# One order of products for all still weights, and one place in SBUF for each kind of weight slab

## The chip, the core and the metric

The kernel runs on one core of a Trainium2 chip. The metric is the device time of one execution in microseconds (us), the median of repeated runs. The core has five engines that work side by side: TensorE (PE) for matrix products, VectorE (DVE), ScalarE (ACT), GpSimd (POOL) and SyncE (SP), which here issues the loads from memory. PE's work shows in the profile as two streams: PEld loads a block of 128x128 weights, PE streams the other operand past the weights that were loaded. The weights' side of a product is called still here, the streamed side moving.

## What is computed

Two transformer-like blocks in a row on one sequence of 256 positions with 1024 channels, batch 1, depth 1, all in float32. Cut to the products that matter:

```python
# first block
h = rms_norm(x, g_mix[i]); proj = h @ w_in[i]          # 1024 x 8192
x = x + mixed @ w_out[i]                                # after attention, retention, two branch products
h2 = rms_norm(x, g_mlp[i])
x = x + jnp.square(jax.nn.relu(h2 @ w_ff1[i])) @ w_ff2[i]          # 1024 -> 4096 -> 1024
gate_p = jax.nn.sigmoid(rms_norm(x, g_ple[i]) @ w_ple_gate[i])
x = x + gate_p * (p[i] @ w_ple[i])
# second block
x = x + mlstm_mixer(rmsnorm(x, l0_norm_mix), ...)       # 1024 -> 3080, mixer, 1024 -> 1024
u = causal_dwconv(x @ w_up, conv_w, conv_b)             # 1024 -> 5632
x = x + (silu(u[..., :2816]) * u[..., 2816:]) @ w_down  # 2816 -> 1024
return rmsnorm(x, final_norm)
```

## The kernel before

**Precision.** Each float32 product is made from three products of a reduced type (fp32r). An operand is split in two: hi is a rounded copy, lo the rest. A product then is hi·hi + hi·lo + lo·hi. Of the input these parts are called xh and xl, of a weight hi and lo. So each block of weights is used three times: hi with xh, hi with xl, lo with xh.

**Slabs.** The weights come in slabs, each of 8 rows of 128 input channels by 256 output channels (two blocks of 128, m = 0 and 1). A slab is loaded in two half slabs of four rows (k = 0 to 3 and 4 to 7). For a half slab SP loads 512 KB into a buffer raw (four of these), ACT rounds it to hi (L198), DVE subtracts to get lo (L208), and PE runs 24 products of 128x128 by 256. hi and lo have six buffers each. A plan lists all half slabs in the order of use, and `slot()`, called after each half slab, lets ACT and DVE split the half slab that is six ahead, and lets the work behind earlier slabs go on a step.

**Two kinds of slabs.** In most of them the weights are still and the input moves (`step_b`, `pe_b`): q, k, qr, kr, ga, gb, wd, wr, wo, f1 (16 slabs), f2 (16), pg, mq, mk, mw, ug and uv (11 each), 98 slabs in all, and wp with a code of its own (L985). In 20 slabs (va, vr, gr, mv, mo) the input is still and the weights move (`step_a`, `pe_a`, L279 to L281; mv0 is wider, L358 to L360). At the end come 11 slabs dn, whose weights move too, 512 or 256 columns at a time (L1406 to L1408).

**The order of the 24 products** of a half slab with still weights differs by slab:
- `pe_b` (L259 to L261): for each m, for each row k, the three kinds one after the other: hi·xh, hi·xl, lo·xh. Interleaved: two hi, then one lo. All slabs but those below.
- f2 through `pe_b2` (L268): for each row, for each kind in the order hi·xh, lo·xh, hi·xl, both m.
- ug and uv from j = 2 (L268 too): for each m, all four rows of hi·xh, then all four of hi·xl, then all four of lo·xh. Eight hi, then four lo.

Joint pairs of slabs, such as f1_0 with f1_1 or mq0 with mk0, where the input is still being made, run rows 0 to 3 of both slabs, then rows 4 and 5 of both, then 6 and 7. The first pair, q0 with k0, goes by two rows throughout.

**Places.** Each buffer of hi and lo is 1088 elements long, of which 1024 are used; `slot_of` shifts the data by 16 elements (64 bytes) times a number from 0 to 3 that `_place` gives for hi and for lo. The buffers are multiples of 256 bytes apart, so the number sets where the data begins modulo 256 bytes: 0, 64, 128 or 192. The inputs (xh, xl) all begin at 0 modulo 256. A pair like (3,1) below means hi at 192 and lo at 64. Before, the f1 slabs, the f2 slabs and ug2 to uv10 go through all sixteen pairs, hi's number running fastest; va and mv stand at (j,0), vr at (j,1), gr at (j,2), mo at (j,3), dn at its own series, and the rest at (3,1):

```python
sh = 16 * _place(name)[tag == "lo"]
t = wpool.tile([P, 1088], F32R, tag=tag, name=f"{tag}_{name}_{s}", bufs=NBUF)
return t[:, sh:sh + kk * pitch].rearrange("p (k n) -> p k n", k=kk)[:, :, 0:cw]
```

Small products (transposes, attention, retention, sums over the channels) stand between some slabs and interrupt the stream. There are such pauses through attention and retention, at the start of most stages, and after uv2 to uv5.

Of the kernel before, what the change touches and what calls it, by code (L numbers as in the profile page):

```python
# [16 lines left out]
P = 128  # L17
T = 256
# [7 lines left out]
NRAWUP = 2  # L26
# [69 lines left out]
def _rows(slab):  # L96

    name, w, k0, nk, cl = slab
    return ((0, 1), (2, 3, 4), (5, 6, 7)) if name == "mv0" else (tuple(range(nk // 2)), tuple(range(nk // 2, nk)))


def _width(slab):
    return 264 if slab[0] == "mv0" else 2048 // slab[3]


def _place(name):

    n, j = name[0:2], int(name[-1]) if name[-1].isdigit() else 0
    if name.startswith("f1_"):
        j = int(name[3:])  # L110
        return j % 4, j // 4
    if name.startswith("f2_"):
        j = 4 * int(name[3]) + int(name[5])
        return j % 4, j // 4
    if n in ("va", "vr", "gr", "mv", "mo"):
        j = (4 * ("va", "vr", "gr", "mo", "mv").index(n) + j) % 16
        return j % 4, j // 4
    if n in ("ug", "uv"):
        j = int(name[2:])
        if j > 1:  # L120
            j = 2 * (j - 2) + (n == "uv")
            return j % 4, j // 4 % 4
    if n == "dn":
        j = int(name[2:])
        return j % 4, (j + j // 4) % 4
    return 3, 1


@with_exitstack
def block_kernel(ctx: ExitStack, tc: tile.TileContext, I, out):  # L130
    nc = tc.nc
    V, S, TE = nc.vector, nc.scalar, nc.tensor
# [7 lines left out]
    def bigt(name, dt=F32, cols=2048):  # L140
        return big.tile([P, 2112], dt, tag="big", name=name)[:, 0:cols]

    def c8(t):
        return t.rearrange("p (c t) -> p c t", t=T)

    def mmbank(name):
        return psum.tile([P, 512], F32, tag="mm", name=name)
# [4 lines left out]
    def wk(name, cols, tag=None, bufs=2, parts=P):  # L152
        return work.tile([parts, cols], F32, tag=tag or name, name=name, bufs=bufs)
# [4 lines left out]
    def pr(ap):  # L158
        return ap.rearrange("p (c t) -> p c t", c=2)
# [3 lines left out]
    raw_t, hi_t, lo_t = {}, {}, {}  # L163
# [5 lines left out]
    def geometry(i):  # L169
        return len(_rows(slabs[i])[0]), _width(slabs[i])  # L170
# [77 lines left out]

    def pe_b(ps, i, xh, xl, ks, m, start, stop):

        kk, cw = geometry(i)
        mc = min(P, cw)
        o = ps[0:mc, m * T:(m + 1) * T]
        for k in ks:
            hv, lv = hi_t[i, k // kk], lo_t[i, k // kk]
            a, x = k % kk, k
            sl = slice(m * P, m * P + mc)
            st, sp = start and k == ks[0], stop and k == ks[-1]
            TE.matmul(o, lhsT=hv[:, a, sl], rhs=xh[:, x, :], start=st, stop=False, skip_group_check=True)  # L259
            TE.matmul(o, lhsT=hv[:, a, sl], rhs=xl[:, x, :], start=False, stop=False, skip_group_check=True)  # L260
            TE.matmul(o, lhsT=lv[:, a, sl], rhs=xh[:, x, :], start=False, stop=sp, skip_group_check=True)  # L261

    def pe_b2(ps, i, xh, xl, ks, start, stop, steps):

        kk, cw = geometry(i)
        for n, (k, m, q) in enumerate(steps):
            wv = (lo_t if q == 2 else hi_t)[i, k // kk]
            TE.matmul(ps[:, m * T:(m + 1) * T], lhsT=wv[:, k % kk, m * P:(m + 1) * P], rhs=(xl if q == 1 else xh)[:, k, :],  # L268
                      start=start and n == 0, stop=stop and n == len(steps) - 1, skip_group_check=True)

    def pe_a(ps, i, xh, xl, ks, t, start, stop):

# [22 lines left out]
    def after(i, *posts):  # L295

        if i in hooks_pe:
            drain(i - 1)
            for f in hooks_pe.pop(i):
                f()  # L300
        slot()
        for f in list(posts) + hooks_post.pop(i, []):
            later(i, f)

    def halves(i, piece):
        for s in range(len(_rows(slabs[i]))):
            need(i, s)
            piece(s)
            used.add((i, s))
            if s == 0:  # L310
                while tails and i >= tails[0][0]:
                    tails.pop(0)[1]()
                if i in hooks_mid:
                    drain(i - 1)
                    for f, g in hooks_mid.pop(i):
                        f()
                        later(i, g)
                slot()

    def step_b(name, xh, xl, post, passes=False):  # L320
        i = index[name]
        ps = mmbank(f"ps_{name}")

        def piece(s):
            if passes:
                ks = range(4 * s, 4 * s + 4)
                pe_b2(ps, i, xh, xl, ks, s == 0, s == 1, [(k, m, q) for m in range(2) for q in range(3) for k in ks])
                return
            for m in range(2):
                pe_b(ps, i, xh, xl, range(4 * s, 4 * s + 4), m, s == 0 and m == 0, s == 1 and m == 1)  # L330

        halves(i, piece)
        after(i, lambda: post(ps))
# [73 lines left out]
    with tc.manual_schedule():  # L407
        S.preload_act_table_set(LNEXP)

        x = bigt("x0")  # L410
# [76 lines left out]
        def split_plain(src, hv, lv):  # L487
            S.activation(hv, src, ACTF.Copy)
            yield
            V.tensor_tensor(out=lv, in0=src, in1=hv.bitcast(F32), op=ALU.subtract)  # L490
# [127 lines left out]
        va = bigt("va").rearrange("p (t n) -> p t n", t=2)  # L618
# [146 lines left out]
        i, ps0 = index["q0"], [mmbank(f"ps_{n}") for n in ("q0", "k0")]  # L765
# [35 lines left out]
        for j in range(2):  # L801
            step_b(f"qr{j}", hhv, hlv, post_scaled(qrt, j, r1))
# [7 lines left out]
        gr, ga = bigt("gr").rearrange("p (t n) -> p t n", t=2), c8(bigt("ga"))  # L810
# [82 lines left out]
        def post_res(key, j, hv, lv, g, r=None):  # L893
            def f(ps):
                xp = xT[:, 2 * j:2 * j + 2, :]
                if r is None:
                    V.tensor_tensor(out=xp, in0=pr(ps), in1=xp, op=ALU.add)
                else:
                    t = wk(f"pr_{key}{j}", 768, tag="lg")[:, 0:512]
                    V.tensor_tensor(out=pr(t), in0=pr(ps), in1=b2(r), op=ALU.mult)  # L900
                    V.tensor_tensor(out=xp, in0=xp, in1=pr(t), op=ALU.add)
                yield
                split_gain(xp, hv, lv, j, lambda c: gcol(g, c))
                later(STAT, lambda: sq_add(key, xp, j))
            return f
# [24 lines left out]
        ah, al = {}, {}  # L930
# [27 lines left out]
        for j in range(4):  # L958
            ps = mmbank(f"ps_f2_{j}")
            for kg in range(4):  # L960
                i = index[f"f2_{j}_{kg}"]

                def piece(s):
                    ks = range(4 * s, 4 * s + 4)
                    pe_b2(ps, i, ah[kg], al[kg], ks, kg == 0 and s == 0, kg == 3 and s == 1,
                          [(k, m, q) for k in ks for q in (0, 2, 1) for m in range(2)])

                halves(i, piece)
                after(i, *([lambda j=j, ps=ps: post_res("n3", j, h3h, h3l, "g_ple", r2)(ps)] if kg == 3 else []))
# [5 lines left out]
        i = index["wp"]  # L975
        need(i, 0)
        need(i, 1)
        for j in range(4):
            ps = mmbank(f"ps_wp{j}")
            for m in range(2):  # L980
                o = ps[:, m * T:(m + 1) * T]
                sl = slice((2 * j + m) * P, (2 * j + m + 1) * P)
                for k in range(2):
                    hv, lv = hi_t[i, k], lo_t[i, k]
# [178 lines left out]
        mc = wk("mc", 8, bufs=1)  # L1163
# [156 lines left out]
        ug, uv = {}, {}  # L1320
# [22 lines left out]
        def post_ug(j):  # L1343
            def f(ps):
                yield from conv(ps, 2 * j, 2 * j, f"g{j}")
                y = ug[j] = pr(ring[:, (2 * j) % 4, :])
                S.activation(y, y, ACTF.Silu)
                if j == NUP - 1:
                    S.preload_act_table_set(LNEXP)
            return f  # L1350

        def post_uv(j):
            def f(ps):
                yield from conv(ps, 22 + 2 * j, 2 * j + 1, f"v{j}")
                y = pr(ring[:, (2 * j + 1) % 4, :])
                V.tensor_tensor(out=y, in0=ug.pop(j), in1=y, op=ALU.mult)
                yield
                b, r = divmod(2 * j, 8)
                if r == 0:
                    gh[b], gl[b] = c8(bigt(f"gh{b}", F32R)), c8(bigt(f"gl{b}", F32R))  # L1360
                yield from split_plain(y, gh[b][:, r:r + 2, :], gl[b][:, r:r + 2, :])
            return f
# [21 lines left out]
        for j in range(1, NUP):  # L1384
            if j == NRAWUP:
                drain(0)
            hv, lv = (h6h, h6l) if j < NRAWUP else (h7h, h7l)
            step_b(f"ug{j}", hv, lv, post_ug(j), j >= NRAWUP)
            step_b(f"uv{j}", hv, lv, post_uv(j), j >= NRAWUP)


        gfb = bigt("gfb")[:, 0:D]
# [175 lines left out]
```

## Time and profile before

| What | us |
|---|---|
| median of 3 runs (791.1 to 791.39) | 791.21 |
| the profiled execution | 790.84 |
| its span, first to last instruction | 789.0 |
| DVE busy | 569.0 |
| ACT busy | 464.7 |
| f2, 768 products (370.7 to 461.1 us of the span) | 90.4 |

The profile counts from the start of the span. An engine's busy time is the union of its instructions, and a product's own duration (some 280 ns) overlaps the next one's, so the pace of PE is read from starts: a window without pauses, divided by the products in it. The DMA engines are busy for 55.6% of the span with the weights.

### The profile page before, as it was taken

How to read it: one execution, taken by the hardware profiler on the slowest of the kernel's cores; microseconds unless marked ns; L12 is line 12 of the kernel's file. 1: busy time of each engine (PE TensorE's matmuls, PEld its weight loads, DVE VectorE, ACT ScalarE, POOL GpSimd, SP SyncE). 2: the span in 40 equal slices, each digit the busy share in tenths (PEclk: the TensorE clock that was granted, in tenths of full speed). 3: DMA queues.
4: the chain of work that ended last, by engine and by line, in shares of the span. 5: the costliest groups of instructions: out<-in, count | busy, mean ns of one | idle time of the engine just before them, and what ended most of it. 6: DMA issues, size and time to landing. Idle time of an engine off the chain costs nothing.

```text
span 789.0 us, 15702 instructions
## 1 busy us (share of the span) xinstructions
PE 777.8 (99%) x6394; PEld 763.1 (97%) x6394; DVE 569.0 (72%) x895; ACT 464.7 (59%) x788; POOL 2.2 (0%) x8
## 2 busy tenths in 40 slices
PE   8999999999999999999999999999999999999996
PEld 8999999999999999999999999999999999999885
DVE  6887889566666668666545557897978988987443
ACT  6665656765744546555344456666866676766432
POOL 0000000000000000000000000000000000000000
PEclk9999999999999999999999999999999999999999
DMA  7775444455666556566666554355365556765631
GB/s 274 260 254 167 150 157 129 158 161 166 195 200 192 183 188 196 187 185 195 191 188 185 188 160 160 135 201 168 122 206 163 164 187 215 237 193 176 196 101 54
DMA packets 40472, 141.75 MB, mean 180 GB/s; under 512 B 4640, under 2 KB 5024, under 8 KB 40400
## 3 DMA queue, kind: packets, MB, share of 16 engines
q1 hardware_dynamic: 40032, 140.02, 55.6%
q8 instruction: 50, 0.82, 0.4%
q0 software_dynamic: 224, 0.72, 0.2%
q14 instruction: 22, 0.18, 0.1%
q10 hardware_dynamic: 144, 0.00, 0.0%
HBM read 139.68 MB, written 1.05 MB: 178 GB/s over the span
## 4 chain that ended last, share of the span: by engine, by line
PE 96%; ACT 1%; DVE 1%; DMA 1%; issue 0%; SPq 0%
PE ps_f L268 11%; PE ps_ug L268 6%; PE ps_uv L268 6%; PE ps_f L259 4%; PE ps_f L260 4%; PE ps_f L261 4%; PE acc L1407 3%; PE acc L1408 3%; PE acc L1406 3%; PE ps_vr L279 1%; PE ps_va L279 1%; PE ps_gr L281 1%; PE ps_va L281 1%; PE ps_mo L281 1%; PE ps_va L280 1%; PE ps_mo L279 1%
## 5 line engine op out<-in xcount | busy, mean ns | idle before, releaser
L208 DVE TENSOR_TENSOR lo_f<-raw_f,hi_f 128x1024 fp32r<-128x1024 f32 x64 | 77.7, 1224 | 52.3 <-ACT hi_f L198 52.3
L198 ACT ACTIVATE hi_f<-raw_f 128x1024 fp32r<-128x1024 f32 x64 | 67.6, 1060 | 78.5 <-PE ps_f L268 36.9
L259 PE MATMUL ps_f<-h2h,hi_f 128*128 128x256 f32 x256 | 72.1, 282 | 0.0
L260 PE MATMUL ps_f<-h2l,hi_f 128*128 128x256 f32 x256 | 71.8, 281 | 0.0
L261 PE MATMUL ps_f<-h2h,lo_f 128*128 128x256 f32 x256 | 71.7, 280 | 0.0
L268 PE MATMUL ps_f<-ah,hi_f 128*128 128x256 f32 x256 | 51.1, 281 | 0.0
L268 PE MATMUL ps_f<-ah,lo_f 128*128 128x256 f32 x256 | 50.9, 280 | 0.0
L268 PE MATMUL ps_f<-al,hi_f 128*128 128x256 f32 x256 | 50.9, 280 | 0.0
L261 PEld LDWEIGHTS ps_f<-h2h,lo_f 128*128 128x128 f32 x256 | 48.3, 189 | 0.0
L259 PEld LDWEIGHTS ps_f<-h2h,hi_f 128*128 128x128 f32 x256 | 48.2, 188 | 0.0
L260 PEld LDWEIGHTS ps_f<-h2l,hi_f 128*128 128x128 f32 x256 | 48.2, 188 | 0.0
L208 DVE TENSOR_TENSOR lo_dn<-raw_dn,hi_dn 128x1024 fp32r<-128x1024 f32 x22 | 26.9, 1224 | 23.3 <-ACT hi_dn L198 23.3
L198 ACT ACTIVATE hi_dn<-raw_dn 128x1024 fp32r<-128x1024 f32 x22 | 23.3, 1060 | 31.2 <-PE acc L1407 24.8
L268 PEld LDWEIGHTS ps_f<-ah,lo_f 128*128 128x128 f32 x256 | 39.3, 189 | 0.0
L268 PEld LDWEIGHTS ps_f<-ah,hi_f 128*128 128x128 f32 x256 | 39.3, 189 | 0.0
L268 PEld LDWEIGHTS ps_f<-al,hi_f 128*128 128x128 f32 x256 | 39.2, 188 | 0.0
L1407 PE MATMUL acc<-hi_dn,gl 128*128 128x512 f32 (+1 forms) x110 | 38.3, 348 | 0.0
L1408 PE MATMUL acc<-lo_dn,gh 128*128 128x512 f32 (+1 forms) x110 | 38.3, 348 | 0.0
L1406 PE MATMUL acc<-hi_dn,gh 128*128 128x512 f32 (+1 forms) x110 | 38.2, 348 | 0.0
L208 DVE TENSOR_TENSOR lo_ug<-raw_ug,hi_ug 128x1024 fp32r<-128x1024 f32 x22 | 26.5, 1221 | 6.0 <-ACT hi_ug L198 6.0
L198 ACT ACTIVATE hi_ug<-raw_ug 128x1024 fp32r<-128x1024 f32 x22 | 22.8, 1052 | 8.5 <-PE ps_uv L268 4.8
L208 DVE TENSOR_TENSOR lo_uv<-raw_uv,hi_uv 128x1024 fp32r<-128x1024 f32 x22 | 26.7, 1219 | 1.2 <-ACT hi_uv L198 1.2
(482 smaller groups left out, 2822.9 us busy)
## 6 DMA issues: line engine op xcount, KB each, us to landing
raw_f<-in_w_dram SPq DMA_DIRECT2D x64, 512.0 KB, 4.1
raw_ug<-in_w_dram SPq DMA_DIRECT2D x22, 512.0 KB, 4.1
raw_uv<-in_w_dram SPq DMA_DIRECT2D x22, 512.0 KB, 4.2
raw_dn<-in_w_dram SPq DMA_DIRECT2D x22, 512.0 KB, 3.6
raw_va<-in_w_dram SPq DMA_DIRECT2D x8, 512.0 KB, 4.4
raw_vr<-in_w_dram SPq DMA_DIRECT2D x8, 512.0 KB, 3.4
raw_gr<-in_w_dram SPq DMA_DIRECT2D x8, 512.0 KB, 3.5
raw_ga<-in_w_dram SPq DMA_DIRECT2D x8, 512.0 KB, 3.7
```

What stands on the lines that cost most here:

```text
L198: S.activation(hi_t[i, s], raw_t[i, s], ACTF.Copy)
L208: V.tensor_tensor(out=lo_t[i, s], in0=raw, in1=hi_t[i, s].bitcast(F32), op=ALU.subtract)
L259: TE.matmul(o, lhsT=hv[:, a, sl], rhs=xh[:, x, :], start=st, stop=False, skip_group_check=True)
L260: TE.matmul(o, lhsT=hv[:, a, sl], rhs=xl[:, x, :], start=False, stop=False, skip_group_check=True)
L261: TE.matmul(o, lhsT=lv[:, a, sl], rhs=xh[:, x, :], start=False, stop=sp, skip_group_check=True)
L268: TE.matmul(ps[:, m * T:(m + 1) * T], lhsT=wv[:, k % kk, m * P:(m + 1) * P], rhs=(xl if q == 1 else xh)[:, k, :], start=start and n == 0, ...
L279: TE.matmul(o, lhsT=xh[:, k, ts], rhs=hv[:, a, :], start=st, stop=False, skip_group_check=True)
L280: TE.matmul(o, lhsT=xl[:, k, ts], rhs=hv[:, a, :], start=False, stop=False, skip_group_check=True)
L281: TE.matmul(o, lhsT=xh[:, k, ts], rhs=lv[:, a, :], start=False, stop=sp, skip_group_check=True)
L1406: TE.matmul(o, lhsT=gh[b][:, r, ts], rhs=hv[:, 0, ns], start=k == 0, stop=False)
L1407: TE.matmul(o, lhsT=gl[b][:, r, ts], rhs=hv[:, 0, ns], start=False, stop=False)
L1408: TE.matmul(o, lhsT=gh[b][:, r, ts], rhs=lv[:, 0, ns], start=False, stop=k == NK - 1)
```

## The change

All slabs with still weights get the order of ug and uv, within each piece of rows that is run at once (four rows, or two in the joint pairs): for each m, hi·xh over the rows, hi·xl over the rows, lo·xh over the rows. `pe_b2` goes away and `pe_b` takes its work. All these slabs stand at (3,1). The slabs with moving weights, dn apart, stand at (3,3). wp, whose products keep their order, goes to (0,2). dn keeps its places.

```diff
 def _place(name):
 
-    n, j = name[0:2], int(name[-1]) if name[-1].isdigit() else 0
-    if name.startswith("f1_"):
-        j = int(name[3:])
-        return j % 4, j // 4
-    if name.startswith("f2_"):
-        j = 4 * int(name[3]) + int(name[5])
-        return j % 4, j // 4
+    n = name[0:2]
     if n in ("va", "vr", "gr", "mv", "mo"):
-        j = (4 * ("va", "vr", "gr", "mo", "mv").index(n) + j) % 16
-        return j % 4, j // 4
-    if n in ("ug", "uv"):
-        j = int(name[2:])
-        if j > 1:
-            j = 2 * (j - 2) + (n == "uv")
-            return j % 4, j // 4 % 4
+        return 3, 3
     if n == "dn":
         j = int(name[2:])
         return j % 4, (j + j // 4) % 4
+    if n == "wp":
+        return 0, 2
     return 3, 1
...
     def pe_b(ps, i, xh, xl, ks, m, start, stop):
 
-        kk, cw = geometry(i)
-        mc = min(P, cw)
-        o = ps[0:mc, m * T:(m + 1) * T]
-        for k in ks:
-            hv, lv = hi_t[i, k // kk], lo_t[i, k // kk]
...
-            TE.matmul(o, lhsT=hv[:, a, sl], rhs=xh[:, x, :], start=st, stop=False, skip_group_check=True)
-            TE.matmul(o, lhsT=hv[:, a, sl], rhs=xl[:, x, :], start=False, stop=False, skip_group_check=True)
-            TE.matmul(o, lhsT=lv[:, a, sl], rhs=xh[:, x, :], start=False, stop=sp, skip_group_check=True)
...
+        kk = geometry(i)[0]
+        o = ps[:, m * T:(m + 1) * T]
+        sl = slice(m * P, (m + 1) * P)
+        steps = [(q, k) for q in range(3) for k in ks]
+        for n, (q, k) in enumerate(steps):
             wv = (lo_t if q == 2 else hi_t)[i, k // kk]
...
+            TE.matmul(o, lhsT=wv[:, k % kk, sl], rhs=(xl if q == 1 else xh)[:, k, :], start=start and n == 0,
+                      stop=stop and n == len(steps) - 1, skip_group_check=True)
...
                 def piece(s):
-                    ks = range(4 * s, 4 * s + 4)
-                    pe_b2(ps, i, ah[kg], al[kg], ks, kg == 0 and s == 0, kg == 3 and s == 1,
-                          [(k, m, q) for k in ks for q in (0, 2, 1) for m in range(2)])
+                    for m in range(2):
+                        pe_b(ps, i, ah[kg], al[kg], range(4 * s, 4 * s + 4), m, kg == 0 and s == 0 and m == 0,
+                             kg == 3 and s == 1 and m == 1)
```

The order on PE at three places, first f1_7, which keeps its place (3,1). These are the last three products of its first half slab and the first three of its second, before (h2h and h2l are xh and xl of the input; ps_f1_7 is the sum):

```order
L259 MATMUL ps_f1_7_4136<-h2h_3379,hi_f1_7_0_3992 128x256
L260 MATMUL ps_f1_7_4136<-h2l_3380,hi_f1_7_0_3992 128x256
L261 MATMUL ps_f1_7_4136<-h2h_3379,lo_f1_7_0_3996 128x256
L259 MATMUL ps_f1_7_4136<-h2h_3379,hi_f1_7_1_4025 128x256
L260 MATMUL ps_f1_7_4136<-h2l_3380,hi_f1_7_1_4025 128x256
L261 MATMUL ps_f1_7_4136<-h2h_3379,lo_f1_7_1_4033 128x256
```

On PE at the same place in the program now, where each row stands for four products, the second m of the first half slab and the first m of the second:

```order
L247 MATMUL ps_f1_7_4136<-h2h_3379,hi_f1_7_0_3992 128x256 x4
L247 MATMUL ps_f1_7_4136<-h2l_3380,hi_f1_7_0_3992 128x256 x4
L247 MATMUL ps_f1_7_4136<-h2h_3379,lo_f1_7_0_3996 128x256 x4
L247 MATMUL ps_f1_7_4136<-h2h_3379,hi_f1_7_1_4025 128x256 x4
L247 MATMUL ps_f1_7_4136<-h2l_3380,hi_f1_7_1_4025 128x256 x4
L247 MATMUL ps_f1_7_4136<-h2h_3379,lo_f1_7_1_4033 128x256 x4
```

One lo after two hi has become four lo after eight hi.

In f2_1_3, also at (3,1), PE had runs of two products, one for each m, here the last of the first half slab and the first of the second (ah12 and al12 are xh and xl):

```order
L268 MATMUL ps_f2_1_5001<-ah12_4568,hi_f2_1_3_0_5059 128x256 x2
L268 MATMUL ps_f2_1_5001<-ah12_4568,lo_f2_1_3_0_5066 128x256 x2
L268 MATMUL ps_f2_1_5001<-al12_4569,hi_f2_1_3_0_5059 128x256 x2
L268 MATMUL ps_f2_1_5001<-ah12_4568,hi_f2_1_3_1_5094 128x256 x2
L268 MATMUL ps_f2_1_5001<-ah12_4568,lo_f2_1_3_1_5096 128x256 x2
L268 MATMUL ps_f2_1_5001<-al12_4569,hi_f2_1_3_1_5094 128x256 x2
```

On PE it now reads:

```order
L247 MATMUL ps_f2_1_5001<-ah12_4568,hi_f2_1_3_0_5059 128x256 x4
L247 MATMUL ps_f2_1_5001<-al12_4569,hi_f2_1_3_0_5059 128x256 x4
L247 MATMUL ps_f2_1_5001<-ah12_4568,lo_f2_1_3_0_5066 128x256 x4
L247 MATMUL ps_f2_1_5001<-ah12_4568,hi_f2_1_3_1_5094 128x256 x4
L247 MATMUL ps_f2_1_5001<-al12_4569,hi_f2_1_3_1_5094 128x256 x4
L247 MATMUL ps_f2_1_5001<-ah12_4568,lo_f2_1_3_1_5096 128x256 x4
```

lo has moved from the middle to the end of each group, and a group runs over rows of one m, not over both m of a row.

In the joint pair mq0 and mk0, where PE follows the making of its input h4h and h4l, rows 4 and 5 and then 6 and 7 are run by two; now PE's rows for mq0 and then mk0, last m of the one and first of the other, are:

```order
L247 MATMUL ps_mq0_6159<-h4h_5830,hi_mq0_1_6031 128x256 x2
L247 MATMUL ps_mq0_6159<-h4l_5831,hi_mq0_1_6031 128x256 x2
L247 MATMUL ps_mq0_6159<-h4h_5830,lo_mq0_1_6035 128x256 x2
L247 MATMUL ps_mk0_6160<-h4h_5830,hi_mk0_1_6064 128x256 x2
L247 MATMUL ps_mk0_6160<-h4l_5831,hi_mk0_1_6064 128x256 x2
L247 MATMUL ps_mk0_6160<-h4h_5830,lo_mk0_1_6072 128x256 x2
```

The second row of h4h is read by the second product of the group; in the interleaved order it was the fourth. No row of ACT, DVE, POOL or SP has moved.

More of the change, by code (lines that the diff above doesn't have):

```diff
@@ L249, in pe_b @@
     def pe_b(ps, i, xh, xl, ks, m, start, stop):
-        kk, cw = geometry(i)
-        mc = min(P, cw)
-        o = ps[0:mc, m * T:(m + 1) * T]
-        for k in ks:
-            hv, lv = hi_t[i, k // kk], lo_t[i, k // kk]
[L256 to L260, printed above, removed]
-            TE.matmul(o, lhsT=lv[:, a, sl], rhs=xh[:, x, :], start=False, stop=sp, skip_group_check=True)
-    def pe_b2(ps, i, xh, xl, ks, start, stop, steps):
-        kk, cw = geometry(i)
-        for n, (k, m, q) in enumerate(steps):
+        kk = geometry(i)[0]
[3 more added lines that the diff above has]
+        for n, (q, k) in enumerate(steps):
             wv = (lo_t if q == 2 else hi_t)[i, k // kk]
-            TE.matmul(ps[:, m * T:(m + 1) * T], lhsT=wv[:, k % kk, m * P:(m + 1) * P], rhs=(xl if q == 1 else xh)[:, k, :],
-                      start=start and n == 0, stop=stop and n == len(steps) - 1, skip_group_check=True)
+            TE.matmul(o, lhsT=wv[:, k % kk, sl], rhs=(xl if q == 1 else xh)[:, k, :], start=start and n == 0,
+                      stop=stop and n == len(steps) - 1, skip_group_check=True)
     def pe_a(ps, i, xh, xl, ks, t, start, stop):
@@ L318, in halves, with step_b @@
                 slot()
-    def step_b(name, xh, xl, post, passes=False):
+    def step_b(name, xh, xl, post):
         i = index[name]
@@ L324, in piece @@
         def piece(s):
-            if passes:
-                ks = range(4 * s, 4 * s + 4)
-                pe_b2(ps, i, xh, xl, ks, s == 0, s == 1, [(k, m, q) for m in range(2) for q in range(3) for k in ks])
-                return
             for m in range(2):
@@ L963, in piece @@
                 def piece(s):
-                    ks = range(4 * s, 4 * s + 4)
-                    pe_b2(ps, i, ah[kg], al[kg], ks, kg == 0 and s == 0, kg == 3 and s == 1,
-                          [(k, m, q) for k in ks for q in (0, 2, 1) for m in range(2)])
+                    for m in range(2):
+                        pe_b(ps, i, ah[kg], al[kg], range(4 * s, 4 * s + 4), m, kg == 0 and s == 0 and m == 0,
+                             kg == 3 and s == 1 and m == 1)
                 halves(i, piece)
@@ L1387, in block_kernel @@
             hv, lv = (h6h, h6l) if j < NRAWUP else (h7h, h7l)
-            step_b(f"ug{j}", hv, lv, post_ug(j), j >= NRAWUP)
-            step_b(f"uv{j}", hv, lv, post_uv(j), j >= NRAWUP)
+            step_b(f"ug{j}", hv, lv, post_ug(j))
+            step_b(f"uv{j}", hv, lv, post_uv(j))
         gfb = bigt("gfb")[:, 0:D]
```

## The prediction

> **What bounds the kernel.** I read the page's busy times first, then the chain that ended last, then what TensorE (PE) waited for.
>
> ```profile
> PE 777.8 (99%) x6394; PEld 763.1 (97%) x6394; DVE 569.0 (72%) x895; ACT 464.7 (59%) x788; POOL 2.2 (0%) x8
> PE 96%; ACT 1%; DVE 1%; DMA 1%; issue 0%; SPq 0%
> ```
> ```profile
> PE ps_q L259 <- ACT hi_q L506: 1.4, 2, 0.8
> PE my L595 <- DVE w_m L584: 1.2, 1, 1.2
> ```
>
> PE is busy for 99% of the span, makes up 96% of the chain, and its two largest waits come to 2.6 us (columns: total us, times, longest). So the time is the number of products times the distance from one start to the next. The change leaves the number alone; only the distance can move. The chain in order of time shows that distance, since it gives each stretch of one line with its length (start us, us, count):
>
> ```profile
> 617.32 5.76 PE ps_ug L268 x48
> 623.08 5.68 PE ps_uv L268 x48
> ...
> 629.19 5.68 PE ps_ug L268 x48
> 634.88 5.55 PE ps_uv L268 x48
> ...
> 640.86 5.70 PE ps_ug L268 x48
> 646.56 5.66 PE ps_uv L268 x48
> ...
> 652.66 5.64 PE ps_ug L268 x48
> 658.30 5.45 PE ps_uv L268 x48
> ...
> 664.18 5.70 PE ps_ug L268 x48
> 669.88 5.54 PE ps_uv L268 x48
> 675.42 5.70 PE ps_ug L268 x48
> 681.12 5.66 PE ps_uv L268 x48
> 686.78 5.65 PE ps_ug L268 x48
> 692.43 5.44 PE ps_uv L268 x48
> 697.87 5.66 PE ps_ug L268 x48
> 703.53 5.65 PE ps_uv L268 x48
> 709.18 5.75 PE ps_ug L268 x48
> 714.93 5.68 PE ps_uv L268 x48
> ```
>
> These are slabs ug2, uv2, ug3 to uv10, all in the order that the change gives to everybody, at the places (hi, lo) = (0,0), (1,0), (2,0), (3,0), (0,1), (1,1), (2,1), (3,1), (0,2) and so on to (3,3), then (0,0), (1,0) again. The same 48 products take 5.76 us at (0,0) and 5.45 us at (3,1), the pair that the change gives to nearly all; only (1,3) is as short, 5.44. In ns per product: 120.0, 113.5, 113.3.
>
> Then windows that cover one stage or one half slab each (columns: window, its length, PE busy with products; the count includes two that reach over the edges; then clock, DMA share, GB/s):
>
> ```profile
> 120.72:123.55 2.83, 2.83 (x26) 1.00 0.54 159
> 562.54:565.44 2.90, 2.90 (x26) 1.00 0.35 138
> 565.44:568.18 2.74, 2.74 (x26) 1.00 0.00 0
> 319.82:322.67 2.85, 2.85 (x26) 1.00 0.63 183
> 322.67:325.53 2.86, 2.86 (x26) 1.00 0.56 186
> 410.48:413.25 2.77, 2.77 (x26) 1.00 0.71 191
> 413.25:415.97 2.72, 2.72 (x26) 1.00 0.66 187
> 605.91:617.32 11.41, 11.41 (x98) 1.00 0.45 143
> ```
> ```profile
> 214.42:279.70 65.28, 65.28 (x578) 65.28 (x578) 43.57 (x51) 33.10 (x39) 0.00 (x0) 1.00 0.59 191
> 297.22:370.69 73.47, 73.47 (x626) 73.47 (x626) 51.26 (x58) 42.46 (x56) 0.00 (x0) 1.00 0.62 194
> 370.70:461.10 90.40, 90.40 (x770) 90.40 (x770) 48.60 (x50) 39.44 (x44) 0.00 (x0) 1.00 0.62 190
> 617.32:720.61 103.29, 103.29 (x881) 103.29 (x881) 93.17 (x142) 68.75 (x100) 0.53 (x1) 1.00 0.64 199
> ```
>
> The last block has all engines (PE, PEld, DVE, ACT, POOL). wd0 to wo3 (214.42) run 576 products in 65.28 us, **113.3 ns each**; f1_3 to f1_15 (297.22) run 624 in 73.47 and f2 (370.70) 768 in 90.40, 117.7 each. The granted clock is 1.00 in all and the DMA share alike, so neither is the cause. But places are not all of it: ug1 and uv1 (605.91) stand at (3,1) in the same interleaved order as wd0, and take 11.41 us for 96, 118.9 ns. So there are **two paces**, a fast one of 113.3 and a slow one of about 118, both stable, and a pause of PE can move it from one to the other. The interleaved order at (3,1) does not leave the slow one: f1_7 takes 2.85, then 2.86 us for 24. Runs of two products per place do: f2_1_3, also (3,1), comes in slow, takes 2.77 and then 2.72, which is 24 times 113.3.
>
> **The change, part by part.** No product, DMA or vector instruction is added or removed; ACT, DVE, POOL and SP keep their order. The profiled execution took 790.84 us, 789.0 of span and 1.84 around it; the median of the runs is 791.21, so I add 0.37 at the end.
>
> (a) f1, 16 slabs: new order and places. The 13 shown go from 73.47 to 624 x 0.1133 = 70.7, or 0.21 us a slab; 16 slabs give 3.4.
>
> (b) f2, 768 products: from 90.40 to 768 x 0.1133 = 87.0, gain 3.4.
>
> (c) ug2 to uv10, 18 slabs, order kept, new places: the rows add up to 101.55; 18 x 5.44 = 97.92, gain 3.6.
>
> (d) Slabs that stand at (3,1) already and change only their order. Those in the slow pace are q1, k2, q3, qr0, qr1, kr0, pg0 to pg3, ug1 and uv1: 12 slabs, at 5.705 each by the 605.91 row, so 12 x 0.265 = 3.2 if all turn fast. Most follow a pause, where each starts slow and needs some products to turn. Those that are fast now (wd to wo and others) have nothing to gain and may lose a little. Bounds 0 and 3.2; I take 2.3, nearer the upper end since f2_1_3 turned within half a slab.
>
> (e) The 20 slabs that stream their weights (va, vr, gr, mv, mo), 40 half slabs, order kept, now all at (3,3). vr1's second half at (1,1) takes 2.83, mo2's at (2,3) 2.90; mo3's first half, the only slab of this kind at (3,3) now, 2.74. So 0.09 to 0.16 each, 3.6 to 6.4 for 40. A pause lies between most of them and may leave some slow; I take 3.3, just under the lower end.
>
> (f) wp moves from (3,1) to (0,2) with its order kept: 48 products, and by the row at 664.18 (5.70 us at (0,2)) it stays within 0.1 of what it is. dn keeps places and order: 0.
>
> (g) Waits. The grouped order wants lo as the ninth product of a half slab, not the third, and xl as the fifth, not the second: both later, so no wait is added there. It frees hi after product 20 of 24, not 23, which is 0.3 us earlier for ACT's next hi:
>
> ```profile
> ACT hi_f L198 <- PE ps_f L260: 32.9, 25, 3.2
> 495.81 0.47 DVE h4l L484
> ```
>
> ACT waits long there, but PE does not wait for ACT, so that is worth 0. In the joint slabs, where the order runs over two rows at a time, the second row of the input is wanted earlier: xh by three products, xl by one. At mq0 PE follows h4l closely (the row at 495.81 is on the chain), so each of the two late groups may cost 0.11 to 0.34, or nothing; I take 0.2 in all. And a faster PE reaches the 1.2 us wait for w_m sooner: what mq, mk and mv gained just before, up to 1 us, may be waited away there; I take 0.5. Behind that wait stand only PE's own next products. Other gains have cover: in wd to wo DVE is busy 43.57 of 65.28 us and raw data comes at 191 GB/s without PE waiting at 113.3, and f1 at that pace would have DVE busy 51.26 of 70.7. The tightest is the ug stage, DVE 93.17 of 103.29 us, to be 99.7: still under.
>
> (h) Starting slow after the pauses of the ug stage and f1: half a slab at 0.2 us, some five times, 0.5.
>
> Sum: 3.4 + 3.4 + 3.6 + 2.3 + 3.3 = 16.0, less 0.2 + 0.5 + 0.5 = 14.8. 790.84 - 14.8 = 776.0, and 776.4 as a median.
>
> **A rule against it.** By the Trainium skill, "TensorE: Matmul & The Clock Gate", section "Step-by-step: what each phase is for", the engine has two independent read ports into SBUF, and loading the next weights takes no bandwidth from the running product. By that rule place and order would be free and the sum 0. The trace disagrees: 5.44 to 5.76 us for the same 48 products, by place alone.
>
> **Rivals.**
>
> 1. *Mixed paces.* Grouping only lets PE turn fast if a change of place comes at the right moment. uv9 at (3,3) holds 5.65 for a whole slab, and no row shows a slow PE in runs of eight hi and four lo. From 291 to 461 us nothing pauses PE, so one slow start could hold through f1 and f2: 6.5 of the gain gone, 782.9. With the ug stage slow instead, 780. For: slow pace is stable. Against: f2_1_3. Chance 0.17, 779.5 to 786.
>
> 2. *Slow everywhere.* If runs of eight and four lock PE in the slow pace from whatever start, every still slab costs what uv9 does, 5.65. Then some 34 slabs that run at 5.44 now (wd to wo 12, ga, gb, mw, parts of q, k, kr, mk and ug) lose 0.21 each, 7.1; the 12 of (d) gain 0.055 each, 0.7; the moving ones gain 0.4; the rest stands still. 790.84 + 6.0 and 0.37: 797.2. It decides from the first pause after which a slab stays at 5.65. Against: uv5 ran 48 products in this order at (3,1) and kept the fast pace. Chance 0.05.
>
> 3. *The paces do not follow the places.* The fast slabs may have been fast by what went before (uv5 and uv8 follow slabs that ended fast), and the new places only deal the paces anew: no change, 791.2. This is also where the page's rule ends. Chance 0.05, against it mo3, uv5, uv8 and f2_1_3, all fast at 3 and 1 only.
>
> 4. *All fast at once*, with (d) and (e) at their full 3.2 and 5 and no loss: 3 us better, 773. Chance 0.03.
>
> **How the numbers follow.** The forecast has 0.70, 774 to 779.5. Low end 773.6, just over rival 4; the high end goes half way into rival 1, 783.5, which leaves 0.2 out. Faster by over 0.2% (about what a measurement of this kernel can tell from no change): forecast, rivals 1 and 4, 0.90; same 0.05; slower 0.05.
>
> **What would show it.** Right: f2 in one stretch of about 87.0 us, each ug and uv slab at 5.44 to 5.5, wd to wo still 65.3, moving half slabs at 2.72 to 2.75, DVE and ACT counts unchanged. A slab in the new order at 5.65 after a pause, and again after the next, speaks for rivals 1 and 2. The forecast is wrong if f1 and f2 keep 117.7 ns a product, or if PE's list of waits grows by more than 2 us.

## The result, and the profile after

The changed kernel takes **778.33 us** (median, 777.9 to 778.93) where the kernel before takes 791.15 (790.74 to 791.39) on the same chip: a ratio of **0.9839, 95% interval 0.9822 to 0.9856**. It is 12.8 us faster. The forecast was 776.4, so the gain is 2 us short of it.

The profiled execution took 777.9 us, with a span of 776.1. First the page's busy times and its chain by engine, then what PE waited for (total us, times, longest):

```profile
PE 764.9 (99%) x6394; PEld 750.1 (97%) x6394; DVE 568.0 (73%) x895; ACT 464.7 (60%) x788; POOL 2.2 (0%) x8
PE 97%; DVE 1%; DMA 1%; ACT 1%; issue 0%; SPq 0%; ACTq 0%
```
```profile
PE ps_q L247 <- ACT hi_q L481: 1.6, 3, 0.7
PE my L570 <- DVE w_m L559: 1.2, 1, 1.2
PE warm L404 <- DVE epst L401: 1.1, 1, 1.1
```

The counts of instructions are those of before, PE's busy time has shrunk by 12.9 us, as the span has, and PE's waits add up to 3.9 us, as they did. So the whole gain is distance between the starts of products. The windows of four stages (window, length, then busy time and count of PE, PEld, DVE, ACT and POOL, clock, DMA share, GB/s), in the order wd0 to wo3, f1_3 to f1_15, f2, and ug2 to uv10 with the small products among them:

```profile
211.81:279.06 67.25, 67.25 (x578) 67.25 (x578) 44.12 (x51) 33.07 (x39) 0.00 (x0) 1.00 0.59 184
295.87:366.58 70.71, 70.71 (x626) 70.71 (x626) 51.24 (x58) 42.53 (x56) 0.00 (x0) 1.00 0.64 201
366.58:453.62 87.04, 87.04 (x771) 87.04 (x770) 48.59 (x49) 39.86 (x45) 0.00 (x0) 1.00 0.63 197
607.03:707.68 100.65, 100.65 (x882) 100.65 (x881) 93.35 (x143) 68.78 (x100) 0.54 (x1) 1.00 0.66 205
```

f1_3 to f1_15 (73.47 before) and f2 (90.40) now run every product at the fast pace of 113.33 ns. But **wd0 to wo3 has lost 1.97 us** (65.28 before), at the same clock and DMA share and with nearly the same vector work (DVE 43.57 us before). The chain in order of time shows the late slabs (start us, us, what):

```profile
607.03 5.44 PE ps_ug L247 x48
612.48 5.45 PE ps_uv L247 x48
617.92 0.44 PE xt L1346 x4
618.36 5.66 PE ps_ug L247 x48
624.01 5.66 PE ps_uv L247 x48
629.67 0.44 PE xt L1346 x4
630.11 5.49 PE ps_ug L247 x48
635.60 5.45 PE ps_uv L247 x48
641.05 0.44 PE xt L1346 x4
641.49 5.66 PE ps_ug L247 x48
647.14 5.66 PE ps_uv L247 x48
652.80 0.44 PE xt L1346 x4
653.24 5.49 PE ps_ug L247 x48
658.73 5.44 PE ps_uv L247 x48
```

All these slabs have the same order, place and shape. Whether one runs in 5.44 or in 5.66 us (117.8 ns a product) goes with the pauses, the four xt products: ug3 starts slow and stays so through uv3 up to the next pause, ug4 starts slow and turns within its first half slab (5.49), ug5 and uv5 stay slow again, and ug6 turns as ug4 did. From uv6 on, behind the last pause, everything runs at 5.44. The last section comes back to this alternation.

Below, **excess** is the distance between the starts of neighbouring products of one kind less 113.33 ns, waits and pauses left out, summed up over the trace of a kernel. Before, it was 14.65 us in the still slabs, 4.71 in the moving ones and 0.26 in wp; now 4.95, 1.67 and 0.01. The difference, 13.0 us, accounts for the 12.9 of the span.

### The profile page after: what moved, and what is told of

It is laid out like the page before. It is cut to its first block, busy times and chain, and to the rows that moved or that the text cites. A ratio compares the mean times of both kernels' runs of the same rounds, so it can differ in the third digit from the quotient of the medians.

```text
span 776.1 us, 15702 instructions
## 1 busy us (share of the span) xinstructions
PE 764.9 (99%) x6394; PEld 750.1 (97%) x6394; DVE 568.0 (73%) x895; ACT 464.7 (60%) x788; POOL 2.2 (0%) x8
## 4 chain that ended last, share of the span: by engine, by line
PE 97%; DVE 1%; DMA 1%; ACT 1%; issue 0%; SPq 0%; ACTq 0%
PE ps_f L247 22%; PE ps_ug L247 8%; PE ps_uv L247 8%; PE ps_wr L247 3%; PE ps_wd L247 3%; PE ps_gb L247 3%; PE ps_wo L247 3%; PE ps_pg L247 3%; PE ps_mw L247 3%; PE ps_ga L247 3%; PE ps_q L247 3%; PE ps_k L247 3%; PE acc L1382 3%; PE acc L1383 3%; PE acc L1381 3%; PE ps_mq L247 2%
## 5 line engine op out<-in xcount | busy, mean ns | idle before, releaser
L247 PE MATMUL ps_f<-h2h,hi_f 128*128 128x256 f32 x256 | 40.3, 277 | 0.0
L247 PE MATMUL ps_f<-h2h,lo_f 128*128 128x256 f32 x256 | 40.1, 276 | 0.0
L247 PE MATMUL ps_f<-h2l,hi_f 128*128 128x256 f32 x256 | 40.1, 276 | 0.0
L247 PE MATMUL ps_f<-ah,lo_f 128*128 128x256 f32 x256 | 39.4, 276 | 0.0
L247 PE MATMUL ps_f<-ah,hi_f 128*128 128x256 f32 x256 | 39.4, 276 | 0.0
L247 PE MATMUL ps_f<-al,hi_f 128*128 128x256 f32 x256 | 39.4, 276 | 0.0
L247 PEld LDWEIGHTS ps_f<-h2h,hi_f 128*128 128x128 f32 x256 | 34.2, 188 | 0.1
L247 PEld LDWEIGHTS ps_f<-h2h,lo_f 128*128 128x128 f32 x256 | 34.1, 188 | 0.0
L247 PEld LDWEIGHTS ps_f<-h2l,hi_f 128*128 128x128 f32 x256 | 34.1, 188 | 0.0
L247 PEld LDWEIGHTS ps_f<-ah,hi_f 128*128 128x128 f32 x256 | 33.8, 188 | 0.0
```

Of the source, the lines that this page charges most:

```text
L247: TE.matmul(o, lhsT=wv[:, k % kk, sl], rhs=(xl if q == 1 else xh)[:, k, :], start=start and n == 0, stop=stop and n == len(steps) - 1, ski ...
```

## Experiments

Theory 1 is the forecast's mechanism with what the profile after adds: PE has a fast and a slow pace, a pause deals which one comes, places allow the fast one or not, and the order of hi and lo decides whether a slow stretch turns fast or is kept until the next pause. The first four kernels ran beside each other (the kernel before: 790.96 us there).

**Places of the change, orders of before.**

```diff
 # the kernel before, with the change's _place
-    if name.startswith("f1_"):
...
     if n in ("va", "vr", "gr", "mv", "mo"):
-        j = (4 * ("va", "vr", "gr", "mo", "mv").index(n) + j) % 16
-        return j % 4, j // 4
+        return 3, 3
...
+    if n == "wp":
+        return 0, 2
     return 3, 1
```

> Places of the change, orders of before (interleaved in most slabs, pairs in f2, eight hi and four lo in ug2 to uv10). Theory 1 (a rhythm: the place of the weights sets what the slow pace costs, and a change of place, at the right moment, lets PE fall into the fast pace): f2 all fast, 87.0 us; f1, interleaved, either all at 113.3 or all at 118.9 ns a product after its one pause, so 87.3 or 91; the whole 778 to 783 us. Theory 2 (the change of order did the work): little gained, 788 to 791. Theory 3 (neither matters, the paces are dealt by pauses alone): anywhere from 778 to 791, with slow slabs at f2 too.

Measured: 783.13 us (783.01 to 783.46), ratio 0.9901 (0.9886 to 0.9916). Windows of f1_3 to f1_15, of f2's first half slab, of the rest of f2, and of wd0 to wo3 (window, length, PE busy, clock, DMA share, GB/s):

```profile
294.17:368.35 74.18, 74.18 (x626) 1.00 0.64 192
368.35:371.09 2.74, 2.74 (x26) 1.00 0.81 247
371.09:455.41 84.32, 84.32 (x747) 1.00 0.62 195
212.00:277.28 65.28, 65.28 (x579) 1.00 0.61 190
```

In the interleaved order, at (3,1), f1 keeps 118.9 ns through all 13 slabs. Then, with no pause between, f2 begins in its own order at the same place: its first half slab needs 2.74 us, and from there 744 products run in 84.32, which is 113.3 each. So at one place the two orders differ: the one kept the slow pace, the other left it. It is not the order alone, though. In the kernel before, k1 has f1's order and place (3,1), and after its pause it turns within six products (the last section has the row). wd0 to wo3 happened to start fast here, and the interleaved order kept that too.

**Orders of the change, places of before.**

```diff
 # the changed kernel, with before's _place
-    if n in ("va", "vr", "gr", "mv", "mo"):
-        return 3, 3
+    if name.startswith("f1_"):
+        j = int(name[3:])
+        return j % 4, j // 4
...
```

> Order of the change, places of before. Theory 1: f1, f2 and ug keep 113.3 to 120 ns by place, as ug2 to uv10 did, so f2 stays near 90 us and the whole comes to 787 to 790. Theory 2: most of the gain, 779 to 783. Theory 3: as for the places alone, 778 to 791.

Measured: 787.8 us (787.73 to 788.24), ratio 0.9962 (0.9948 to 0.9976). f1_3 to f1_15 and f2:

```profile
296.42:369.44 73.02, 73.02 (x627) 1.00 0.61 195
369.44:459.57 90.13, 90.13 (x770) 1.00 0.63 190
```

Both stages are within half a microsecond of before. The order alone brings 3.2 us, the places alone 7.8, both together 12.8.

**All still slabs at (0,0), and all at (3,3).**

```diff
 # in _place of the changed kernel
-    return 3, 1
+    return 0, 0      # the other kernel: return 3, 3
```

> The changed kernel with all still slabs but wp at (0,0) and not (3,1). Theory 1: each still product costs 120.0 ns as in ug2 before, against a mean of 114.4 now: 4704 x 5.6 ns = 26 us more, 804 us, and no fast slab among them. Theory 3: no difference, 778 us.

> The changed kernel with all still slabs but wp at (3,3) and not (3,1), so that hi and lo begin at the same place and no product changes place. Theory 1: nothing lets a slow PE turn fast, so nearly all still slabs run at 117.7 ns as uv9 did before: up to 4704 x 3.3 ns = 15 us more, 790 to 794 us; fast stretches only from one pause to the next. A rival in which hi at 192 alone makes it fast: 778 us, as now.

Measured: 803.55 us (803.42 to 803.88) at (0,0), ratio 1.0159 (1.0144 to 1.0174); 792.07 (791.73 to 792.5) at (3,3), ratio 1.0014 (1.0004 to 1.0023). wd0 to wo3, first at (0,0), then at (3,3):

```profile
216.85:285.97 69.12, 69.12 (x578) 1.00 0.57 177
```
```profile
213.06:280.91 67.85, 67.85 (x579) 1.00 0.59 180
```

576 products take 120.0 ns each at (0,0), and there every one of the still half slabs does. At (3,3) nearly all run at 117.8, with a few fast stretches that begin and end at pauses: where hi and lo have the same place nothing turns a slow start, and it stays. With order and work alike, the numbers in `_place` alone are worth 25 us, from (3,1) to (0,0).

The next four ran together (the kernel before: 791.18 us).

**The passes over two rows at a time** (four hi, two lo) in all still slabs, where the change takes four rows:

```diff
-        steps = [(q, k) for q in range(3) for k in ks]
+        steps = [(q, k) for r in range(0, len(ks), 2) for q in range(3) for k in ks[r:r + 2]]
```

> The changed kernel with the passes of every slab with still weights taken over two rows at a time (four products with hi, two with lo, twice in a half slab) where the change takes all four rows (eight with hi, four with lo). Places and everything else as in the change. Theory 1 (a pause deals the products one of two paces, 113.33 or 117.78 ns; eight and four keep the slow one from one pause to the next in places, while four and two turn it to the fast one within about a half slab): the stretch from the last gb slabs to wo1, the late ug and uv pairs and q and k come to 113.3 ns; their excess over 113.33 ns in the changed kernel was about 5 us in all still slabs, of which 3.4 to 3.7 us go: 774.6 us (774 to 775.5). Rival A (the slow stretches come from what other engines do to the memory of the core at that time, so the order of products can't end them): 778.3 us, with the same stretches at 117.8 ns. Rival B (it was the number of changes from hi to lo that cost: twice as many here): 44 slabs with 4 more changes each, slower than the change, 779 to 781 us.

**The same in one slab only, wd0**, the first of the long slow stretch:

```diff
+        by = 2 if slabs[i][0] == "wd0" else len(ks)
-        steps = [(q, k) for q in range(3) for k in ks]
+        steps = [(q, k) for r in range(0, len(ks), by) for q in range(3) for k in ks[r:r + by]]
```

> The changed kernel, and the passes over two rows at a time in the one slab wd0 (eight half-slab groups), which stands at the beginning of the slow stretch of wd, wr and wo; every other slab as in the change. Theory 1 (pace is kept from one pause to the next, and the order of products turns it): wd0 begins at 117.8 ns and is at 113.3 at its end, and wd1 to wo0, whose code is not touched, run at 113.3 as well: 1.8 to 2.0 us less than the change, 776.4 us. Rival A (traffic of other engines in that stretch): wd1 to wo0 stay at 117.8, and the time is 778.3 us. Rival C (each slab's own order alone sets its pace): only wd0 gains, about 0.2 us: 778.1 us.

Measured: 775.25 us for all slabs (774.57 to 775.45), ratio 0.9796 (0.9782 to 0.981), and **776.4 for wd0 alone** (775.94 to 776.54), ratio 0.9812 (0.9798 to 0.9826). In the latter the two halves of wd0, and then wr0 to wo3, whose code is untouched:

```profile
211.97:214.74 2.77, 2.77 (x26) 1.00 0.68 244
214.74:217.46 2.72, 2.72 (x26) 1.00 0.08 33
217.46:277.30 59.84, 59.84 (x530) 1.00 0.62 194
```

wd0 turns within its first half slab, and the 528 products behind it run at 113.3 ns. For comparison the first 408 products of the slow stretch of the change, wd0 to the first half of wo0:

```profile
211.81:259.86 48.05, 48.05 (x410) 1.00 0.62 191
```

They run at 117.8 ns, with the same DMA share and nearly the same GB/s as the fast stretch above, so traffic isn't the cause. Another order in one slab, which by itself gains 0.2 us, brings 1.9. With two rows in all slabs the excess of the still slabs falls from 4.95 to 1.44 us.

**The two places changed over** (still slabs at 64 and 192, order of the change):

```diff
 # in _place of the changed kernel
-    return 3, 1
+    return 1, 3
```

> The changed kernel with the slabs with still weights at the places 64 (hi) and 192 (lo) in place of 192 and 64: the two places changed over, the order of products as in the change. Theory 1 with the pace tied to which phase the change from hi to lo meets: here the turn goes the other way round and the slow pace isn't kept by eight and four: about 3.4 us less, 774.8 us (774 to 776). Rival (the two places do the same for hi and lo, only that both are used counts): 778.3 us, slow stretches of the same kind after pauses. If the slow pace is kept everywhere here: up to 791 us as with 192 and 192.

Measured: **774.65 us** (774.22 to 774.93), ratio 0.9791 (0.9777 to 0.9804). The late slabs in the chain, ug3, uv3 and ug4, uv4:

```profile
616.29 5.46 PE ps_ug L247 x48
621.75 5.44 PE ps_uv L247 x48
627.19 0.44 PE xt L1346 x4
627.63 5.46 PE ps_ug L247 x48
633.09 5.45 PE ps_uv L247 x48
```

After each of these pauses PE is fast almost at once. The excess of the still slabs is 0.98 us, less than in any kernel above.

**The changed kernel once more.**

> The changed kernel once more, not altered, for a second profile of it and a time beside the three others on the same chip. Theory 1 with a pace that is dealt by each pause and depends on the same delays every time: the same slabs (the last gb, wd to wo0, ug3 and uv3, ug5 and uv5) are slow again, 778.3 us. Theory 1 with a pace dealt by chance: other stretches are slow, 776.5 to 780 us. Traffic (rival A): the same slabs, 778.3 us.

Measured: 778.35 us (778.12 to 778.61), ratio 0.9838 (0.9824 to 0.9852), and the same slabs are slow as in the first profile, but for the first half slabs of mq0 and mk0 (some 0.2 us together). So what a pause deals is, in these two profiles, nearly all fixed by the program and not by chance.

**The orders of before, with still slabs at 64 and 192** (moving slabs and wp as in the change; the kernel before took 790.82 us in this job and in the next kernel's):

```diff
 # the kernel before, with the change's _place and in it
-    return 3, 1
+    return 1, 3
```

> The kernel before with all its orders of products (rows one after the other with two hi and one lo, f2's and the late slabs' own), and the places of the change with hi and lo changed over: still weights 64 and 192, moving 192 and 192, wp 0 and 128. Theory 1 as the runs so far shape it (at 192 and 64 the order of two hi and one lo kept f1 at 118.9 ns, because its change meets the same phase each time; with the places changed over it meets another): no still slab stays slow, f1 at 113.3 from its first or second slab on, 774.0 to 775.0 us, so the passes of the change aren't needed. Rival D (two hi and one lo keep the slow pace at any two places, the passes are what turns it): f1 and the other slabs of that order slow as with places 192 and 64 and the old orders, 783 us.

Measured: 774.74 us (774.5 to 774.93), ratio 0.9796 (0.9782 to 0.9809); f1_3 to f1_15:

```profile
293.01:363.73 70.72, 70.72 (x626) 1.00 0.64 201
```

The order that held f1 at 118.9 ns with hi at 192 and lo at 64 turns it fast with hi at 64 and lo at 192. Rival D falls: it is the pair of order and places that keeps the slow pace, neither alone. And the change's new order isn't needed for the gain, the other pair of places does it with the old code.

**The moving slabs back at the places of before.**

```diff
 # in _place of the changed kernel
     if n in ("va", "vr", "gr", "mv", "mo"):
-        return 3, 3
+        j = (4 * ("va", "vr", "gr", "mo", "mv").index(n) + int(name[2:])) % 16
+        return j % 4, j // 4
```

> The changed kernel with the 20 moving-weight slabs back at the places that they have in the kernel before (spread over 0 to 192); still slabs and orders as in the change. Predicted term (e), which was 3.3 us and measures 3.04 us from the starts of products in the two profiles: 781.4 us (781.0 to 781.6), the moving slabs at 117 to 121 ns again and the still slabs as in the change. Rival (the moving products' pace comes from what they follow, so a fast neighbourhood makes them fast at any place): 778.3 to 779 us.

Measured: 778.51 us (778.18 to 779.17), ratio 0.9843 (0.983 to 0.9857): by the time, a miss of 2.9 us. wd0 to wo3, then the second halves of mo2 and of vr1:

```profile
213.62:278.90 65.28, 65.28 (x578) 1.00 0.61 190
...
554.08:556.99 2.91, 2.91 (x27) 1.00 0.31 118
119.46:122.28 2.82, 2.82 (x26) 1.00 0.49 168
```

The moving slabs did lose what was expected: their excess is back at 4.69 us, 3.0 more than in the change. But the pauses among the gb slabs now deal otherwise (gb0 and gb2 are slow, gb1 and gb3 turn fast), wd0 comes in fast, and the stretch to wo0 is at 113.3 again; the last section shows what changed them over. The excess of the still slabs fell from 4.95 to 2.52. So two edits can't be told apart by time in a kernel whose still slabs keep what they are dealt. Hence the same edit in the kernel with places 64 and 192, which keeps nothing, beside that kernel itself (the kernel before: 790.87 us):

> The changed kernel with still weights at 64 and 192 (where no still slab kept the slow pace) and the 20 moving-weight slabs back at the places of the kernel before. The run with the spread moving slabs and still slabs at 192 and 64 came to 778.51 us and not to 781.4: its moving slabs were 3.0 us slower, as expected, but the stretch from wd0 to wo0 was dealt the fast pace this time and gave 2.0 us back. Theory 1: with still slabs that always turn fast nothing can be given back, so the price of the spread places shows in the time: 774.65 + 3.0 = 777.7 us (777.3 to 778.0). Rival (the moving slabs' slow products are made good elsewhere): 774.7 to 775.2 us.

> Still weights at 64 and 192, moving slabs at 192 and 192, orders of the change: the fastest kernel so far once more, beside the one with spread moving slabs on the same chip. 774.65 us (774.2 to 775.0), if its pace doesn't hang on what the pauses deal, as theory 1 says; a time over 776 us would show that it does.

Measured: 777.56 us (776.93 to 777.58) with the spread places, ratio 0.983 (0.9816 to 0.9843), and 774.33 (774.1 to 774.44) without, ratio 0.979 (0.9777 to 0.9804). The difference is 3.2 us, and the fastest kernel is confirmed: 16.5 us under the kernel before, 4 under the change.

## Why the prediction was right, and where it fell short

**What bounds the kernel** and **two paces, by place, order and pause**: right. PE's counts and waits stayed as they were, and in every run the stages that gained or lost did so by the distance between starts. One reading behind the two paces is too wide: that the interleaved order at (3,1) doesn't leave the slow one. In the profile that it was read from, f1, q1 and ug1 keep it, but k1, q2 and gb0 leave it within six products of a pause.

**(a), (b): f1 and f2**, forecast 3.4 and 3.4. The 13 slabs and f2 came to 70.71 and 87.04 us, as worked out (70.7 and 87.0); by excess f1 gained 3.5, f2 3.4. The slow start that rival 1 feared did come: f1_2's second half begins slow after its pause, and it turned before f1_3. (That pause, two small products, stands at 293.8 us before, so the stretch without one began there and not at 291.)

**(c): ug2 to uv10**, forecast 3.6 less a part of (h). The ten rows above and eight more of 5.44 add up to 98.92 us, from 101.55: a gain of 2.6. What is missing is ug3, uv3, ug5 and uv5 at 5.66, 0.22 each, and the first half slabs of ug4 and ug6.

**(d) is the step that failed.** Its first half held: the 12 slabs that were slow at (3,1) gained 2.6 us of excess (2.3 forecast). Its other half said that the slabs that were fast "have nothing to gain and may lose a little", and took the loss as nothing; wd to wo was to be "still 65.3". They lost 2.7: wd, wr and wo 1.97, gb1 and gb3 0.43, k1 0.19, others 0.15. Net, with 0.4 us gained in the joint pair mq0 and mk0 and in a few half slabs besides, (d) gave about 0.2 in place of 2.3. The reason is the one that rival 1 named, in another stretch: from the pause ahead of gb3 to wo0 there is no further pause, the slow start held through all of it, and only the second joint group of wo0 and wo1, which goes by two rows, ended it. With the passes by two rows in all slabs wd to wo came back to 65.28 us. The forecast had the evidence that runs of two turn (f2_1_3), and no row that eight and four do; it gave them the same power. (h) priced a pause at half a slab, 0.1 us; where the pace is kept the price is the whole stretch to the next pause.

**(e): moving slabs**, forecast 3.3: 3.04 by excess, 3.2 by the last pair of runs. Here are the second halves of vr1 and mo2 (2.83 and 2.90 before) and of gr1, which stayed slow:

```profile
118.41:121.13 2.72, 2.72 (x27) 1.00 0.43 128
553.02:555.74 2.72, 2.72 (x27) 1.00 0.48 181
147.27:150.10 2.83, 2.83 (x28) 1.00 0.29 41
```

At (3,3) the fast pace is allowed, but not every slow start turns: gr1, vr2 and vr3 keep 117.8 ns from one pause to the next, while mo1's first distances are 117, 118, 122, 116 and 114 ns, then 113. 1.7 us of excess remain in these slabs.

**(f): wp**, forecast within 0.1: it gained 0.25, since it runs at 113.4 ns here. The place (0,2) is not the reason: in the kernel with all still slabs at (3,3), wp stands at (0,2) too, and its 48 products take 5.70 us, 118.8 ns each, as in the row of ug6 that the forecast went by:

```profile
453.47:458.91 5.44, 5.44 (x50) 1.00 0.58 176
```
```profile
462.08:467.78 5.70, 5.70 (x50) 1.00 0.64 187
```

The first row is the change, the second the kernel at (3,3). wp goes on at the pace at which f2 hands over, and the forecast took that for a property of the place.

**(g): waits**, forecast 0.7 lost: nothing. PE's list of waits adds up to 3.9 us in both profiles. The wait for w_m was to swallow some of what mq, mk and mv gain before it; they gained 0.7 us of excess (mq and mk 0.37, mv 0.38), and the wait is still 1.2. That DVE was done earlier too is likely, but not shown.

**The sum.** 14.8 was forecast and 12.9 came in the span: (c) 1.0 short, (d) 2.1, (e) 0.3; (a) 0.1 and (f) 0.25 better, and of the 1.2 for (g) and (h) nothing shows apart, since what (h) stood for is counted in the slabs above. The error is the size of one term, and behind it one piece of the mechanism: which orders turn the pace.

**Rivals.** Rival 2 (slow everywhere) and rival 3 (the paces don't follow the places) fall: the late slabs turn, and (0,0) with everything else alike costs 25 us. Rival 1 (mixed paces) came true in part. Rival 4 did not come, and its own terms add up to 3.8 us (0.9 + 1.7 + 1.2), not 3; nothing else hangs on that. By the Trainium skill, "TensorE: Matmul & The Clock Gate", section "Step-by-step: what each phase is for", loading the next weights takes no read bandwidth from the product that runs. Read as the forecast reads it, that the place of the weights is free, it doesn't hold here: on PE the still weights are read by that loading alone, and moving hi by 192 and lo by 64 bytes changes the distance between starts from 120.0 to 113.3 ns. Whether the loading takes something from the running product, or is itself slower at some places, no run here shows.

## What to carry to other kernels

Where a core is bound by back-to-back products, read their distance in windows by stage, and compare equal work at different addresses: here the places alone were worth 7.8 us and the order alone 3.2, and the best set of places tried gave 16 us with the old orders. A stable slow pace is priced by the stretch to the next pause, not by the slab in which it starts; so ask of each order whether it gets out of a slow start, and not only whether it can run fast. And where a pace is dealt by what went before, an edit moves time in places that it doesn't touch, so its own price is taken from its own stage or from a kernel that doesn't keep the pace.

## What the runs showed of the hardware that was not expected

The distances from one start to the next, in ns, over the products of half a slab, read from the start times in the trace; a bar marks each change between hi and lo:

```
before, k1 first half, after its pause (2 hi | 1 lo), turned:
 205 118 | 122 | 117 116 | 114 | 113 114 | 113 | 113 114 | 113 | 113 114 | 113 | 113 114 | 113 | 113 114 | 113 | 113 114 | 113
before, ug1 first half (2 hi | 1 lo), kept slow:
 117 125 | 118 | 117 119 | 117 | 118 124 | 118 | 118 118 | 118 | 117 124 | 119 | 117 118 | 118 | 117 125 | 118 | 117 119 | 117
change, wr0 first half (8 hi | 4 lo), kept slow:
 117 118 118 117 118 118 118 118 | 118 117 118 118 | 117 118 118 118 117 119 117 118 | 118 117 118 118
change, gb0 first half, after its pause, turned:
 204 117 118 118 118 117 118 115 | 116 123 118 113 | 114 113 113 114 113 113 114 113 | 113 114 113 113
change, gb1 first half, after its pause, kept slow:
 204 118 118 118 117 118 118 118 | 118 117 118 118 | 118 117 118 118 117 119 117 119 | 117 118 117 118
wd0 by two rows, first half (4 hi | 2 lo), turned:
 118 117 119 114 | 117 120 | 119 116 118 124 | 116 114 | 113 114 113 113 | 115 112 | 113 114 113 113 | 114 113
places 64 and 192, ug3 first half, after its pause, turned:
 207 118 114 113 113 114 113 113 | 114 113 113 114 | 113 114 113 113 113 114 113 113 | 114 113 113 114
still slabs at (0,0), wd1 first half:
 120 120 120 120 120 120 120 120 | 120 120 120 120 | 120 120 120 120 120 120 120 120 | 120 120 120 120
```

The fast pace repeats 113, 113, 114: 340 ns for three products. The slow one comes to 353.3 for three, and (0,0) to a steady 120.0. gb0 and gb1 run the same code at the same places, each after a pause of four small products; from the last product of the slab before to the second of the new one it is 675 ns at gb0 and 679 at gb1. The first change from hi to lo sends the one to the fast pace and leaves the other.

Those few ns are not the whole of it, for ug4 turned after 679 ns. What goes with the outcome is the pace ahead of the pause. In five profiles (two of the change, and one each of wd0 alone by two rows, the moving slabs spread, and the places alone) 36 such pauses of four small products stand ahead of a gb slab or of ug3 to ug6 that goes by eight and four at (3,1). All 36 slabs begin slow. The 15 that follow a slow slab all turn, after 677 to 679 ns. Of the 21 that follow a fast one 18 stay slow, after 678 to 680 ns, and the three that turn are gb0 at 675. So fast and slow alternate from pause to pause, and one pause that falls otherwise changes over all that follow. That is what the spread moving slabs did: gb0 came after 679 ns in place of 675 and stayed slow, gb1 turned, gb2 stayed slow, gb3 turned, and wd0 came in fast. Why a slow slab is followed by one that turns isn't shown.

The rows fit a slow pace that goes through three points in turn, where it matters at which of them a change of place falls: in runs of eight and four it is met every twelve products, a multiple of three, so a change that does nothing once does nothing again. But two and one come round every three products and four and two every six, and four and two left the slow pace all the same, so the period alone can't be the reason. This reading is argued from the distances, and no run tests it alone. What is shown: with hi at 192 and lo at 64, two hi and one lo kept the slow pace (f1, 118.9 ns) or left it (k1), eight and four kept it or left it, four and two left it; with hi at 64 and lo at 192, two and one left it, and eight and four too. Why three, and what in the chip the places contend for, stays open (no run moves the inputs from 0), and so does whether any place and order turns every slow start of the moving slabs.
